# Key-by-receptance products of a delta-rule branch made once, before the solve, and read back from DRAM; output tiles reordered; recurrence one tile later

## The chip, the cores and the metric

One core of one Trainium2 chip. The metric is the device time of one execution in microseconds (us). The core has a matrix engine (PE, whose weight loads are listed as PEld), DVE (vector), ACT (scalar), POOL (GpSimd) and SP, which here only issues DMAs; ACT issues DMAs too.

## The reference

Two layers of a hybrid encoder trunk over 1024 prompt tokens and 8 samples of 16 tokens, T = 1152 tokens in all. In each layer one projection of the normalised input, `z = rmsnorm(x) @ W_in` (1024 to 24 tiles of 128 columns), feeds four branches: A (RWKV-7 time mixing, 4 heads of 64), B (latent attention), C (spatial gating) and D (trailing means); their outputs are gated and go through `W_out`. The change lies in branch A:

```python
def step(s, inp):                       # s: 64 x 64 state of a head
    r_t, w_t, k_t, v_t, kk_t, a_t = inp
    sa = einsum('bhij,bhj->bhi', s, -kk_t)
    s = s * w_t + sa (x) (kk_t * a_t) + v_t (x) k_t
    return s, einsum('bhij,bhj->bhi', s, r_t)
```

## The kernel before, in words

Tokens stand in three groups g of 384 columns; the last group ends with the samples. `project` makes one output tile f of W_in: per group 24 matmuls 128x384 (8 pieces of the contraction, 3 passes of split float32), so 72 for a tile. They read `xh`, `xl` and the weights `wh`, `wl` and fill one of two PSUM buffers `pj`. Below, n is the number of projection matmuls of the layer issued so far: tile number x 72. `F_ORDER` gives the order of the tiles. Behind each group a sink on ACT and DVE takes `pj` away: the token shift of the key, receptance and value tiles (K0, K1, R0, R1, V0, V1: two heads each), `windows` and `silu` for branch D (D0, GD0, D1, GD1).

All else is written as generators that wait in lanes. `tick()` advances each lane by one step, at the places `ticks` within a group and at its end. A scheduler then fixes one order of instructions for each engine, and an engine keeps to its order: what waits holds up all that stands behind it.

Branch A replaces the scan by 18 chunks of 64 tokens, 0 to 15 of the prompt, 16 and 17 of the samples:
- `a_elem(i, g)` makes, for head pair i, the tiles `kb` (both kinds of key divided by decay) and `ar` (the negated key times decay, and the decay, which `receptance` multiplies by r later).
- `systems(g)` makes for each chunk the key-by-key products (`pn`, 4 matmuls 64x64x64, listed as 8 each of 64x64), masks them on DVE into `ns` (two buffers) and writes them to DRAM, `nd` or `nds`, with a DMA on ACT (L514, L515).
- `solve()` loads them in another layout (L528, L529), inverts the unit triangular matrices in a long row of DVE pairs (L538, L540; first 15 pairs for the samples, then 31 pairs for the prompt), and writes the inverses to `dd` (L552, L553, on ACT).
- `recurrence()` goes through chunks 16, 17, 0, 1, ... 15. `prepare(c)` loads the inverse `tt` on SP, makes the key-by-receptance products (four 64x128x128 matmuls into `pg`, 8 listed), masks them on DVE into `Gm` (two buffers, L580), and makes all that does not need the state; `pz` (tt x Gm) is its first product on an inverse. `advance(c)` takes the state through the chunk.

The first 64 columns of the key-by-receptance product, which come from `ar`'s negated key, hold the key-by-key products.

Of the kernel before, what the change touches and what calls it, by code (L numbers as in the profile page):

```python
# [31 lines left out]
(WDAD, K0, R0, V0, K1, R1, V1, D0, GD0, D1, GD1, VC0, VC1, U0, GC0, U1, GC1,  # L32
 GB0, GB1, Q0, Q1K, CK, GA0, GA1) = range(NF)

F_ORDER = (WDAD, K0, K1, R0, R1, V0, V1, D0, GD0, D1, GD1, VC0, VC1, U0, GC0, U1, GC1,
           Q0, Q1K, CK, GB0, GB1, GA0, GA1)


# [10 lines left out]
def tile_trunk(ctx: ExitStack, tc: tile.TileContext, *aps):  # L49
# [60 lines left out]
    def s_tile(tag, bufs, cols=G):  # L110
        return sp_.tile([128, cols], F32, tag=tag, name=nm(tag), bufs=bufs)
# [7 lines left out]
    def pb():  # L119
        return ps_b.tile([128, 512], F32, tag="b", name=nm("b"))  # L120
# [36 lines left out]
    def gcols(g):  # L157
        return slice(g * G, (g + 1) * G)
# [163 lines left out]
    def halves(name, n, cols):  # L322
        return dr.tile([n, 128 * cols + 64], F32, tag=name, name=nm(name))
# [21 lines left out]
    for l in range(L):  # L345
# [13 lines left out]

        def inproj(f, sink):  # L360
            ticks = (3,)
            if f in (K1, R0, R1, V0, V1, D0, GD0, D1, GD1, VC0, VC1, GC0, U1, GC1,
                     GA0, GA1):
                ticks = (2, 5)
            elif f in (U0, GB0, GB1):
                ticks = (1, 3, 5)
            project([(l, f)], xh, xl, [sink], ticks)

# [36 lines left out]
        def shifted(f, dest, after=None):  # L405
            inproj(f, shift_sink(f, dest, after))
# [17 lines left out]
        def chv(t):  # L424
            return t.rearrange("p (c s) -> p c s", s=64)
# [63 lines left out]
        def receptance(i, fr):  # L489
            def after(g, zs):  # L490
                ex = AR[i][g][:, :, 1, :]
                Po.tensor_tensor(out=ex, in0=chv(zs), in1=ex, op=ALU.mult)
            shifted(fr, lambda g: s_tile("gn", 3), after)

        def values(fv):
# [2 lines left out]
            vfm.append(v)  # L498


        nd, nds = halves(f"nd{l}", 32, 64), halves(f"nds{l}", 4, 64)

        def hp(h):
            return slice(64 * (h % 2), 64 * (h % 2) + 64)

        def systems(g):
            for cl in range(6):
                c = 6 * g + cl
                pn = pb()[:, 0:128].rearrange("p (i t) -> p i t", i=2)
                for h in range(4):  # L510
                    mm(pn[hp(h), h // 2, :], KB[h // 2][g][hp(h), cl, h % 2, :], AR[h // 2][g][hp(h), cl, 0, :])
                ns = chp.tile([128, 2, 64], F32, tag="u0", name=nm("ns"), bufs=2)
                mk = cm[:, C_MP if c < 16 else C_MS, 0:64]
                V.tensor_tensor(out=ns, in0=pn, in1=mk.unsqueeze(1).broadcast_to([128, 2, 64]), op=ALU.mult)  # L514
                A.dma_start(out=whole(nd, c, 64) if c < 16 else whole(nds, c - 16, 64),  # L515
                            in_=ns.rearrange("p i t -> p (i t)"))
                if cl % 2:
                    yield

        def solve():  # L520
            NT = m_tile(1024).rearrange("p (s t) -> p s t", s=32)
# [38 lines left out]
        def prepare(c):  # L560

            g, cl = divmod(c, 6)
            samp = c >= 16
            if c == 16:
                St["Ss"] = m_tile(1024).rearrange("p (i s v) -> p i s v", i=2, s=NS)
                SY.dma_start(out=St["Ss"], in_=S0[l])
            tt = chp.tile([128, 2, 128], F32, tag="tt", name=nm("tt"), bufs=2)
            if samp:
                SY.dma_start(out=tt[:, :, 0:64], in_=whole(dds, c - 16, 64).rearrange("x s (i t) -> x s i t", i=2))
            else:  # L570
                SY.dma_start(out=tt.rearrange("p i t -> p (i t)"), in_=whole(dd, c, 128))

            Gm = chp.tile([128, 2, 2, 128], F32, tag="gm", name=nm("gm"), bufs=2)
            for hh in range(2):
                pg = pb()[:, 0:256].rearrange("p (i t) -> p i t", i=2)
                pr = slice(64 * hh, 64 * hh + 64)
                for i in range(2):
                    mm(pg[:, i, :], KB[i][g][pr, cl].rearrange("p a t -> p (a t)"),
                       AR[i][g][pr, cl].rearrange("p a t -> p (a t)"))
                V.tensor_tensor(out=Gm[:, hh], in0=pg,  # L580
                                in1=cm[:, C_MS if samp else C_MP, :].unsqueeze(1).broadcast_to([128, 2, 128]),
                                op=ALU.mult)

            pt = pb()
            for i in range(2):
                PE.transpose(pt[:, i * 128:(i + 1) * 128], KB[i][g][:, cl].rearrange("p a t -> p (a t)"), ident)  # L586
            for i in range(2):
                PE.transpose(pt[0:64, 256 + i * 128:256 + (i + 1) * 128], vfm[i][:, c * 64:(c + 1) * 64], ident)  # L588
            kbt = chp.tile([128, 256], F32, tag="kbt", name=nm("kbt"), bufs=2)
            A.activation(out=kbt, in_=pt[:, 0:256], func=AF.Copy)  # L590
            pvv = pt[0:64, 256:512].rearrange("p (i x v) -> p i x v", i=2, x=2)
            vu = chp.tile([128, 4, 64], F32, tag="vu", name=nm("vu"), bufs=2)
            vuv = vu.rearrange("p (i x) v -> p i x v", x=2)
            for hh in range(2):
                A.activation(out=vuv[64 - 64 * hh:128 - 64 * hh, :, hh, :], in_=pvv[:, :, hh, :], func=AF.Copy)
            yield

            if samp:
                if c == 16:

                    pys = pb()
                    pv4 = pys.rearrange("p (i s a t) -> p i s a t", i=2, s=NS, a=2)
                    for s in range(NS):
                        for h in range(4):
                            rhs = AR[h // 2][2][hp(h), 4 + s // 4, :, 16 * (s % 4):16 * (s % 4) + 16]
                            mm(pv4[hp(h), h // 2, s], St["Ss"][hp(h), h // 2, s, :], rhs)
                    ysm = m_tile(512)
                    St["YS"] = YS = ysm.rearrange("p (i a t) -> p i a t", i=2, a=2)
                    for a in range(2):
                        A.activation(out=YS[:, :, a, :].rearrange("p i (s t) -> p i s t", s=NS),  # L610
                                     in_=pv4[:, :, :, a, :], func=AF.Copy)
                yield
            else:
                pz = pb()
                for h in range(4):
                    o = 64 * (h % 2)
                    mm(pz[o:o + 64, h // 2 * 32:h // 2 * 32 + 32], Gm[o:o + 64, h % 2, h // 2, 0:64],
                       tt[o:o + 64, h // 2, 64:96])
                A.activation(out=zt[:, 0:64], in_=pz[:, 0:64], func=AF.Copy)
                yield  # L620
            pmv = pb()[:, 0:128].rearrange("p (i v) -> p i v", i=2)
            for h in range(4):
                q = slice(64 - 64 * (h % 2), 128 - 64 * (h % 2))
                mm(pmv[hp(h), h // 2, :], Gm[q, h % 2, h // 2, 0:64], vu[q, h, :])
            if not samp:
                pt2 = pb()
                for h in range(4):
                    o = 64 * (h % 2)
                    mm(pt2[o:o + 64, h // 2 * 32:h // 2 * 32 + 32], zt[o:o + 64, h // 2 * 32:h // 2 * 32 + 64],
                       tt[o:o + 64, h // 2, 32:64])  # L630
                for hh in range(2):
                    o = 64 * hh
                    A.activation(out=tt[o:o + 32, :, 32:64],
                                 in_=pt2[o:o + 32, 0:64].rearrange("p (i t) -> p i t", i=2), func=AF.Copy)
            u0 = chp.tile([128, 2, 64], F32, tag="u0", name=nm("u0"), bufs=2)
            A.activation(out=u0, in_=pmv, func=AF.Copy)
            St[c] = (tt, Gm, kbt, vu, u0)
# [266 lines left out]

        def after_k1(g, zs):
            start("a", a_elem(1, g, zs))
            if g > 0:
                go("a", systems(g - 1))

        project([(l, WDAD), (l, K0)], xh, xl,  # L910
                [shift_sink(WDAD, lambda g: z6[:, gcols(g)], tanh_part),
                 shift_sink(K0, lambda g: zk0[:, gcols(g)], lambda g, zs: start("a", a_elem(0, g, zs)))])
        shifted(K1, lambda g: zk1[:, gcols(g)], after_k1)
        go("a", idle(4))
        go("a", systems(2))
        go("a", idle(4))
        go("a", solve())
        receptance(0, R0)
        receptance(1, R1)
        values(V0)  # L920
        values(V1)
        A.dma_start(out=shift_o[l], in_=sho)
        pool_in(0, D0)
        go("a", recurrence())
        pool_gate(0, GD0)
        pool_in(1, D1)
        pool_gate(1, GD1)
        gating()
# [634 lines left out]
```

## Time and profile before

| | us |
|---|---|
| median of 3 runs | 1454.72 (1450.95 to 1456.58) |
| profiled execution | 1454.34 |
| its span | 1452.5 |
| PE busy in the span | 1373.0 (95%) |
| DVE / ACT / POOL busy | 783.5 / 740.7 / 437.7 |

The profiled execution is 1.8 us longer than its span, and its mean granted TensorE clock is 0.987 of full. Times in a trace count from the span's start. Layer 0's branch A stands between 50 and 361 us; layer 1 repeats it some 716 us later.

### The profile page before, as it was taken

To read this page: it belongs to the slowest core of one execution; us is meant where nothing else is said; L and a number is where in the kernel's file an instruction comes from. 1 tells how busy PE (TensorE), PEld (TensorE's weight loads), DVE (VectorE), ACT (ScalarE), POOL (GpSimd) and SP (SyncE) were. 2 spreads that over 40 slices of the span, in tenths; PEclk is the share of its full clock that TensorE was granted. 3 is DMA by queue.
4 is the path that set the end of the run, shared out by engine and by line. 5 is a ranking of instruction groups with operands and counts; after the bars stand their busy time and mean duration, and the time that the engine had idled before them with its cause. 6 is when DMAs were issued, how large, how long until landed. Compare 5 with 4: busy or idle time off the path is not lost. (4 is left out here: it accounts for less than half of the span.)

```text
span 1452.5 us, 26772 instructions
## 1 busy us (share of the span) xinstructions
PE 1373.0 (95%) x9938; PEld 1154.8 (80%) x9938; DVE 783.5 (54%) x1762; ACT 740.7 (51%) x1985; POOL 437.7 (30%) x576
## 2 busy tenths in 40 slices
PE   4899889999999999999989998999999999999999
PEld 3678878888988876679977787788799788666998
DVE  6985944445236557742287858543532474767211
ACT  6772244555366667642257521555643776666210
POOL 4514414336411110322162333332652111112320
PEclk9999999999999999999989999999999999999999
DMA  7213241110312114033301123221022111131232
GB/s 221 52 34 79 56 102 49 56 45 31 103 34 77 53 35 132 3 119 98 88 22 30 50 64 71 85 71 48 31 74 66 58 57 54 44 102 44 70 98 76
DMA packets 116594, 97.38 MB, mean 67 GB/s; under 512 B 46128, under 2 KB 111344, under 8 KB 116464
## 3 DMA queue, kind: packets, MB, share of 16 engines
q1 hardware_dynamic: 76776, 73.74, 17.6%
q10 hardware_dynamic: 39688, 21.94, 5.0%
q8 instruction: 78, 1.28, 0.4%
q14 instruction: 52, 0.43, 0.1%
HBM read 71.48 MB, written 24.16 MB: 66 GB/s over the span
## 5 line engine op out<-in xcount | busy, mean ns | idle before, releaser
L76 PE MATMUL pj<-xh,wh 128*128 128x384 f32 x1152 | 413.8, 360 | 18.0 <-ACT xh L280 7.3
L76 PE MATMUL pj<-xl,wh 128*128 128x384 f32 x1152 | 395.5, 343 | 3.7 <-POOL xl L282 2.7
L76 PE MATMUL pj<-xh,wl 128*128 128x384 f32 x1152 | 395.4, 343 | 0.0
L242 POOL TENSOR_TENSOR wl<-wr,wh 128x256 fp32r<-128x256 f32 x200 | 156.2, 789 | 463.8 <-ACT wh L241 387.5
L76 PEld LDWEIGHTS pj<-xh,wh 128*128 128x128 f32 x1152 | 220.7, 192 | 40.7 <-ACT sho L400 10.0
L76 PEld LDWEIGHTS pj<-xl,wh 128*128 128x128 f32 x1152 | 221.1, 192 | 11.2 <-POOL xl L282 4.7
L76 PEld LDWEIGHTS pj<-xh,wl 128*128 128x128 f32 x1152 | 220.7, 192 | 6.1 <-issue 4.8
L76 PE MATMUL pj<-yh,wh 128*128 128x384 f32 x384 | 130.0, 339 | 2.7 <-DVE x L1386 2.7
L76 PE MATMUL pj<-yh,wl 128*128 128x384 f32 x384 | 129.2, 337 | 0.0
L76 PE MATMUL pj<-yl,wh 128*128 128x384 f32 x384 | 129.0, 336 | 0.0
L241 ACT ACTIVATE wh<-wr 128x256 fp32r<-128x256 f32 x200 | 80.9, 414 | 86.0 <-PE pj L76 41.5
L76 PEld LDWEIGHTS pj<-yh,wh 128*128 128x128 f32 x384 | 72.5, 189 | 4.0 <-DVE x L1386 3.0
L242 POOL TENSOR_TENSOR wl<-m,wh 128x256 fp32r<-128x256 f32 x56 | 43.6, 788 | 103.7 <-ACT wh L241 76.4
L76 PEld LDWEIGHTS pj<-yl,wh 128*128 128x128 f32 x384 | 72.6, 189 | 0.1
L76 PEld LDWEIGHTS pj<-yh,wl 128*128 128x128 f32 x384 | 72.6, 189 | 0.1
L1261 ACT ACTIVATE X<-b,ng 128x512 f32<-128x512 f32 (+3 forms) x96 | 55.0, 576 | 28.7 <-DVE ng L1253 25.0
L76 PEld LDWEIGHTS st<-X,X 128*64 128x64 f32 x576 | 35.5, 136 | 31.6 <-DVE mx L1249 6.3
L76 PE MATMUL b<-sp,cr 128*128 128x384 f32 (+3 forms) x192 | 59.2, 389 | 1.0 <-POOL sp L99 0.6
L1249 DVE TENSOR_REDUCE mx<-b 128x1 f32<-128x512 f32 (+3 forms) x96 | 53.0, 552 | 8.5 <-PE b L76 6.9
L1382 DVE TENSOR_TENSOR pt<-pj,pt 128x384 f32<-128x384 f32 x24 | 13.4, 557 | 80.6 <-PE pj L76 80.6
L241 ACT ACTIVATE wh<-m 128x256 fp32r<-128x256 f32 x56 | 22.5, 413 | 62.2 <-PE pj L76 61.1
L76 PE MATMUL st<-X,X 128*64 128x128 f32 x576 | 53.3, 283 | 0.3
(296 smaller groups left out, 2558.1 us busy)
## 6 DMA issues: line engine op xcount, KB each, us to landing
wr<-in_win_dram SPq DMA_DIRECT2D x176, 128.0 KB
m<-in_wout_dram SPq DMA_DIRECT2D x12, 512.0 KB
x<-in_xT_dram SPq DMA_DIRECT2D x12, 384.0 KB
ysp<-m ACTq DMA_DIRECT2D x24, 192.0 KB
pt<-in_xT_dram SPq DMA_DIRECT2D x24, 192.0 KB
ea<-ysp SPq DMA_DIRECT2D x24, 192.0 KB
x1d<-x ACTq DMA_DIRECT2D x24, 192.0 KB
pt<-x1d SPq DMA_DIRECT2D x24, 192.0 KB
```

What stands on the lines that cost most here:

```text
L76: return PE.matmul(out, lhsT=lhsT, rhs=rhs, start=start, stop=stop, skip_group_check=True)
L241: A.activation(out=h, in_=r, func=AF.Copy)
L242: Po.tensor_tensor(out=lo, in0=r, in1=h.bitcast(F32), op=ALU.subtract)
L1249: V.tensor_reduce(out=mx[:, b:b + 1], in_=pc[:, :w], axis=AX.X, op=ALU.max)
L1261: A.activation(out=P[:, :w], in_=pc[:, :w], func=AF.Exp, scale=SCALE, bias=ng, accum_out=sums[pr][:, b, s, h:h + 1])
L1382: V.tensor_tensor(out=xr, in0=ps, in1=xr, op=ALU.add)
```

## The change

`systems(g)` now makes the whole key-by-receptance product of each chunk, masks it into `Gm`, writes its key-by-key part to `nd`/`nds` (two DMAs, one for each half) and the whole (256 KB) to a new DRAM tile `gd`, all three on SP. `prepare(c)` loads `Gm` from there on SP. The `pn` products, their mask and their DMA on ACT are gone. As the product needs `ar` with r in it, `systems(g)` starts behind `receptance(1, R1)`, one chunk for each step of the lane. To have r early the tiles are reordered: K0, V0, R0, K1, R1, V1 in place of K0, K1, R0, R1, V0, V1. The recurrence enters its lane after GD0 in place of before it, and D1 and GD1 get a third tick.

```diff
-F_ORDER = (WDAD, K0, K1, R0, R1, V0, V1, D0, GD0, D1, GD1, VC0, VC1, U0, GC0, U1, GC1,
+F_ORDER = (WDAD, K0, V0, R0, K1, R1, V1, D0, GD0, D1, GD1, VC0, VC1, U0, GC0, U1, GC1,
...
         def receptance(i, fr):
             def after(g, zs):
                 ex = AR[i][g][:, :, 1, :]
                 Po.tensor_tensor(out=ex, in0=chv(zs), in1=ex, op=ALU.mult)
+                if i == 1:
+                    go("a", systems(g))
...
+        gd = dr.tile([18, 128, 512], F32, tag=f"gd{l}", name=nm("gd"))
...
         def systems(g):
             for cl in range(6):
                 c = 6 * g + cl
-                pn = pb()[:, 0:128].rearrange("p (i t) -> p i t", i=2)
-                for h in range(4):
-                    mm(pn[hp(h), h // 2, :], KB[h // 2][g][hp(h), cl, h % 2, :], AR[h // 2][g][hp(h), cl, 0, :])
-                ns = chp.tile([128, 2, 64], F32, tag="u0", name=nm("ns"), bufs=2)
-                mk = cm[:, C_MP if c < 16 else C_MS, 0:64]
-                V.tensor_tensor(out=ns, in0=pn, in1=mk.unsqueeze(1).broadcast_to([128, 2, 64]), op=ALU.mult)
-                A.dma_start(out=whole(nd, c, 64) if c < 16 else whole(nds, c - 16, 64),
-                            in_=ns.rearrange("p i t -> p (i t)"))
-                if cl % 2:
-                    yield
+                samp = c >= 16
+                Gm = chp.tile([128, 2, 2, 128], F32, tag="gm", name=nm("gm"), bufs=2)
+                mk = cm[:, C_MS if samp else C_MP, :]
+                for hh in range(2):
+                    pg = pb()[:, 0:256].rearrange("p (i t) -> p i t", i=2)
+                    pr = slice(64 * hh, 64 * hh + 64)
+                    for i in range(2):
+                        mm(pg[:, i, :], KB[i][g][pr, cl].rearrange("p a t -> p (a t)"),
+                           AR[i][g][pr, cl].rearrange("p a t -> p (a t)"))
+                    V.tensor_tensor(out=Gm[:, hh], in0=pg, in1=mk.unsqueeze(1).broadcast_to([128, 2, 128]),
+                                    op=ALU.mult)
+                for hh in range(2):
+                    half = nds[2 * (c - 16) + hh] if samp else nd[2 * c + hh]
+                    SY.dma_start(out=half[0:128 * 64].rearrange("(s i t) -> s i t", s=64, i=2),
+                                 in_=Gm[64 * hh:64 * hh + 64, hh, :, 0:64])
+                SY.dma_start(out=gd[c], in_=Gm.rearrange("p h i t -> p (h i t)"))
+                yield
...
             Gm = chp.tile([128, 2, 2, 128], F32, tag="gm", name=nm("gm"), bufs=2)
-            for hh in range(2):
-                pg = pb()[:, 0:256].rearrange("p (i t) -> p i t", i=2)
-                pr = slice(64 * hh, 64 * hh + 64)
-                for i in range(2):
-                    mm(pg[:, i, :], KB[i][g][pr, cl].rearrange("p a t -> p (a t)"),
-                       AR[i][g][pr, cl].rearrange("p a t -> p (a t)"))
-                V.tensor_tensor(out=Gm[:, hh], in0=pg,
-                                in1=cm[:, C_MS if samp else C_MP, :].unsqueeze(1).broadcast_to([128, 2, 128]),
-                                op=ALU.mult)
+            SY.dma_start(out=Gm.rearrange("p h i t -> p (h i t)"), in_=gd[c])
...
-        shifted(K1, lambda g: zk1[:, gcols(g)], after_k1)
-        go("a", idle(4))
-        go("a", systems(2))
-        go("a", idle(4))
-        go("a", solve())
-        receptance(0, R0)
-        receptance(1, R1)
-        values(V0)
+        values(V0)
+        receptance(0, R0)
+        shifted(K1, lambda g: zk1[:, gcols(g)], after_k1)
+        receptance(1, R1)
+        go("a", solve())
         values(V1)
         A.dma_start(out=shift_o[l], in_=sho)
         pool_in(0, D0)
-        go("a", recurrence())
         pool_gate(0, GD0)
+        go("a", recurrence())
         pool_in(1, D1)
         pool_gate(1, GD1)
```

What it does to the order of instructions, at three places of layer 0 (the first number of a row is its place on its engine; line numbers of the changed kernel are 11 higher in the solve and 3 higher behind it).

PE in `systems`, before (some 290 projection matmuls of the layer have been issued): `b` is the PSUM tile of `pn`, two chunks in a row.

```order
299 L76 MATMUL pj_1046<-xh_332,wl_708 128x384
300 L76 MATMUL b_1098<-ar_564,kb_563 64x64 x2
301 L76 MATMUL b_1098<-ar_847,kb_846 64x64 x2
302 L76 MATMUL b_1106<-ar_564,kb_563 64x64 x2
303 L76 MATMUL b_1106<-ar_847,kb_846 64x64 x2
304 L76 MATMUL pj_1114<-xh_405,wh_663 128x384
```

PE in `systems` in the changed kernel, near n = 450: `b` is now `pg`, two of them for a chunk.

```order
452 L76 MATMUL b_1300<-ar_442,kb_441 128x128
453 L76 MATMUL b_1300<-ar_1025,kb_1024 128x128
454 L76 MATMUL pj_1336<-xh_406,wl_971 128x384
455 L76 MATMUL pj_1336<-xh_406,wh_970 128x384
456 L76 MATMUL b_1304<-ar_442,kb_441 128x128
457 L76 MATMUL b_1304<-ar_1025,kb_1024 128x128
458 L76 MATMUL pj_1336<-xl_407,wh_970 128x384
459 L76 MATMUL pj_1336<-xh_406,wl_971 128x384
460 L76 MATMUL pj_1336<-xh_406,wh_982 128x384
461 L76 MATMUL pj_1336<-xl_407,wh_982 128x384
462 L76 MATMUL pj_1336<-xh_406,wl_983 128x384
463 L76 MATMUL b_1325<-ar_442,kb_441 128x128
```

The products come 160 matmuls later in the layer, are two of 128 columns for each half of a chunk, and stand in smaller groups between the projections.

DVE at the end of the solve, before: L538 and L540 are its last pair, L655 is a step of sample chunk 16, L759 the last step of `silu` and L666 the sample chunks' masks.

```order
294 L538 TENSOR_TENSOR m_1395<-m_1394,m_1393 128x31
295 L540 TENSOR_TENSOR m_1394<-m_1394,m_1395 128x31
296 L550 COPY m_1393<-m_1394 128x1024
297 L655 TENSOR_TENSOR u_380_1954<-b_1956,u_380_1954 128x128
298 L580 TENSOR_TENSOR gm_1964<-b_1965,cm 128x256
299 L759 TENSOR_TENSOR pt_1940<-pj_1856,pt_1940 128x384
300 L580 TENSOR_TENSOR gm_1964<-b_1969,cm 128x256
301 L820 SCALAR_TENSOR_TENSOR m_1717<-st_1945,vcs,pt_1940 128x384
302 L759 TENSOR_TENSOR pt_2045<-pj_1983,pt_2045 128x384
303 L820 SCALAR_TENSOR_TENSOR m_1717<-st_2050,vcs,pt_2045 128x384
304 L666 TENSOR_SCALAR m_2000<-vu_1886,mseq_t 128x256 x4
```

DVE at the same place in the changed kernel, where L549 and L551 are the last pair, L794 is a window of D1, L669 the sample chunks' masks and L762 the last step of `silu`:

```order
318 L549 TENSOR_TENSOR m_1724<-m_1723,m_1722 128x31
319 L551 TENSOR_TENSOR m_1723<-m_1723,m_1724 128x31
320 L561 COPY m_1722<-m_1723 128x1024
321 L794 SCALAR_TENSOR_TENSOR m_2049<-pt_2169,pinv_t,m_2048 64x384
322 L794 SCALAR_TENSOR_TENSOR m_2049<-pt_2171,pinv_t,m_2048 64x384
323 L794 SCALAR_TENSOR_TENSOR m_2049<-pt_2286,pinv_t,m_2048 64x384
324 L794 SCALAR_TENSOR_TENSOR m_2049<-pt_2288,pinv_t,m_2048 64x384
325 L794 SCALAR_TENSOR_TENSOR m_2049<-pt_2434,pinv_t,m_2048 64x256
326 L794 SCALAR_TENSOR_TENSOR m_2049<-pt_2436,pinv_t,m_2048 64x256
327 L794 SCALAR_TENSOR_TENSOR m_2049<-pt_2445,pinv_t,zsm_2050 64x128
328 L669 TENSOR_SCALAR m_2188<-vu_2080,mseq_t 128x256 x4
```

Before, the windows of branch D that fell into the solve (those of D0) were worked between its pairs. Now eight windows of D1 stand behind its end, ahead of the masks of chunk 16 (L669).

PE at the end of the solve, before, from the last sample product on an inverse to the first prompt one (`b<-tt,gm`), and the projections that follow:

```order
747 L588 MATMUL b_2071<-cm,m_1373 64x128
748 L588 MATMUL b_2071<-cm,m_1544 64x128
749 L76 MATMUL b_2097<-u_395_2037,tt_1962 64x64 x4
750 L76 MATMUL b_2109<-tt_2060,gm_2062 64x32 x4
751 L76 MATMUL pj_2081<-xh_405,wh_1679 128x384
752 L76 MATMUL pj_2081<-xl_406,wh_1679 128x384
753 L76 MATMUL pj_2081<-xh_405,wl_1680 128x384
754 L76 MATMUL pj_2081<-xh_405,wh_1697 128x384
```

PE at the same place in the changed kernel, at n = 768 (between the second and third group of GD1):

```order
904 L76 MATMUL b_2269<-tt_2237,gm_2239 64x32 x4
905 L76 MATMUL b_2292<-m_2264,kbt_2153 64x256 x4
906 L76 MATMUL b_2300<-gm_2146,vu_2155 64x64 x4
907 L76 MATMUL b_2300<-m_2122,cm 64x64 x4
908 L76 MATMUL b_2311<-vu_2248,gm_2239 64x64 x4
909 L76 MATMUL b_2316<-tt_2237,zt 64x32 x4
910 L589 MATMUL b_2342<-cm,kb_441 128x128
911 L589 MATMUL b_2342<-cm,kb_1024 128x128
912 L591 MATMUL b_2342<-cm,m_738 64x128
913 L591 MATMUL b_2342<-cm,m_1430 64x128
914 L76 MATMUL b_2364<-u_456_2323,tt_2237 64x64 x4
915 L76 MATMUL pj_2719<-xh_406,wh_1981 128x384
```

Before, 45 projection matmuls stand between the solve's last pair and the first prompt product, with the steps of chunks 16 and 17 among them. Now what is left of chunks 16 and 17 and the whole of chunk 0's first steps stand in 23 rows that hold no projection (892 to 914); 8 chunks follow with 4 to 7 projection matmuls between their steps, and the rest with about 24 each, as before.

## Rows read from the trace of the kernel before

**Rows 1.** The page: span, and busy time of each engine.
```profile
span 1452.5 us, 26772 instructions
...
PE 1373.0 (95%) x9938; PEld 1154.8 (80%) x9938; DVE 783.5 (54%) x1762; ACT 740.7 (51%) x1985; POOL 437.7 (30%) x576
```

**Rows 2.** Windows of layer 0: length, then busy time (x instructions) of each engine.
```profile
67.71:162.73 95.02, 88.01 (x549) 75.55 (x548) 70.35 (x173) 42.38 (x112) 29.74 (x41) 0.99 0.21 56
...
177.64:202.37 24.73, 18.37 (x159) 15.45 (x156) 15.18 (x39) 6.95 (x22) 2.06 (x4) 0.93 0.43 80
```

**Rows 3.** The same view for `pj` instructions alone; the second stretch is pure projection.
```profile
67.71:162.73 95.02, 74.33 (x384) 66.83 (x384) 10.95 (x22) 11.53 (x38) 0.99 0.21 56
...
650.00:700.00 50.00, 50.00 (x290) 50.00 (x289) 6.69 (x12) 0.00 (x0) 1.00 0.36 101
```

**Rows 4.** PE groups of 67.71:162.73: count, busy us, mean ns, idle before.
```profile
L76 PE MATMUL b<-ar,kb 64*64 64x64 f32 x144 | 7.9, 228 | 2.2 <-DVE ns L514 1.9 <-DVE kb L481 0.3
...
L76 PE MATMUL st<-m,wlo 64*128 64x384 f32 x8 | 3.6, 535 | 0.0
...
L76 PE MATMUL st<-ea,cr 128*128 128x384 f32 x8 | 3.4, 511 | 0.0
...
L76 PE MATMUL b<-m,wlo 64*128 64x384 f32 x5 | 2.6, 594 | 0.0
```

**Rows 5.** What PE waited for, whole run: us, times, longest.
```profile
PE b L76 <- DVE gm L580: 6.2, 4, 2.9
```

**Rows 6.** PE timeline, two chunks of `systems` between projections: start, us.
```profile
121.44 0.34 PE L76 MATMUL pj<-xh,wl 128*128 128x384 f32 x1
...
121.71 0.68 PE L76 MATMUL b<-ar,kb 64*64 64x64 f32 x16
...
122.32 0.45 PE L76 MATMUL pj<-xh,wh 128*128 128x384 f32 x1
...
122.61 0.34 PE L76 MATMUL pj<-xl,wh 128*128 128x384 f32 x1
```

**Rows 7.** PE timeline, one chunk of the recurrence in its later part.
```profile
300.02 0.45 PE L76 MATMUL b<-vu,kbt 128*64 128x64 f32 x8
...
302.84 0.72 PE L76 MATMUL b<-ar,kb 64*128 64x128 f32 x8
...
303.49 0.44 PE L586 MATMUL b<-cm,kb 128*128 128x128 f32 x2
...
308.01 0.45 PE L76 MATMUL b<-vu,kbt 128*64 128x64 f32 x8
```

**Rows 8.** DVE timeline, the mask of the key products, two chunks apart.
```profile
119.50 0.29 DVE L514 TENSOR_TENSOR ns<-b,cm 128x128 f32<-128x128 f32 x1 [1.46 <-DMA nd<-ns]
...
123.01 0.29 DVE L514 TENSOR_TENSOR ns<-b,cm 128x128 f32<-128x128 f32 x1 [1.56 <-DMA nd<-ns]
```

**Rows 9.** DVE group of the masks in the recurrence.
```profile
L580 DVE TENSOR_TENSOR gm<-b,cm 128x256 f32<-128x256 f32 x72 | 28.3, 417 | 6.6 <-PE b L76 6.6
```

**Rows 10.** ACT timeline, the issue of one 192 KB write.
```profile
358.66 0.33 ACTq L899 DMA_DIRECT2D ysp<-m  x1
```

**Rows 11.** DMA view of 355:362, 40 slices of 0.175 us: what the engines moved.
```profile
GB/s 0 0 0 0 0 0 0 0 0 0 0 0 0 0 0 0 0 0 0 0 0 0 0 0 0 61 377 377 290 65 94 0 0 0 0 0 0 0 0 0
```

**Rows 12.** The tile `nd`, 90:140: ns minimum, median, maximum of the issue.
```profile
L515 ACTq DMA_DIRECT2D nd<-ns x16: 487/502/1078, 98.5 to 128.5; - x16
```

**Rows 13.** Timelines of four engines: the solve, from load to first use.
```profile
132.73 0.62 SPq L528 DMA_DIRECT2D m<-nd  x1
...
184.44 0.22 DVE L540 TENSOR_TENSOR m<-m,m 128x31 f32<-128x31 f32 x1
...
189.25 1.48 ACTq L553 DMA_DIRECT2D dd<-m  x1
...
201.78 0.37 PE L76 MATMUL b<-tt,gm 64*64 64x32 f32 x8
```

**Rows 14.** Windows: the stretch right behind an idle PE.
```profile
183.00:186.40 3.40, 3.34 (x15) 0.50 0.26 29
```

More of the change, by code (lines that the diff above doesn't have):

```diff
@@ L361, in inproj @@
             ticks = (3,)
-            if f in (K1, R0, R1, V0, V1, D0, GD0, D1, GD1, VC0, VC1, GC0, U1, GC1,
+            if f in (K1, R0, R1, V0, V1, D0, GD0, VC0, VC1, GC0, U1, GC1,
                      GA0, GA1):
                 ticks = (2, 5)
-            elif f in (U0, GB0, GB1):
+            elif f in (D1, GD1, U0, GB0, GB1):
                 ticks = (1, 3, 5)
@@ L906, in after_k1 @@
             start("a", a_elem(1, g, zs))
-            if g > 0:
-                go("a", systems(g - 1))
         project([(l, WDAD), (l, K0)], xh, xl,
@@ L923, in tile_trunk @@
         pool_in(0, D0)
+        pool_gate(0, GD0)
         go("a", recurrence())
-        pool_gate(0, GD0)
         pool_in(1, D1)
```

## The prediction

> **What bounds the kernel now.** I read the page first. PE is busy for 1373.0 of 1452.5 us, DVE and ACT for little more than half [rows 1], so the span is PE's row of instructions with its holes, and every edit is priced by what it adds to that row or to a hole in it. Busy time alone misleads: a matmul's record overlaps the next. In pure projection 290 of them fill 50 us, so one costs 50 / 290 = 0.172 us [rows 3], whatever its record says. Then I went to the stretches of layer 0 that the change touches, and read each as its length less its projections. From 67.71 to 162.73 us (n = 144 to 528) there are 384 projections, 66.2 of 95.0 us [rows 2, 3]; 28.8 us are something else. From 177.64 to 202.37, around the end of the solve, PE is busy for 18.37 of 24.73 us, so it is idle for 6.4, the largest hole of the layer [rows 2]. The two layers have the same shapes; I price one and double it.
>
> **1. The key products go.** Between the projections that start at 121.44 and 122.61 lie two chunks of them. Two projections of that 1.17 us are 0.34, so two chunks cost 0.82 and one 0.41 [rows 6]; 18 cost **7.4 us** a layer. Their busy time, 7.9 us [rows 4], says the same. Their DVE mask and DMA go too; neither engine bounds PE there beyond the wait in step 3.
>
> **2. The receptance products move.** One chunk takes PE from 302.84 to 303.49, 0.65 us, in the recurrence [rows 7]. In `systems` it takes the same, but it stands alone between projections, where the first matmul behind a group holds its place for 0.29 us instead of 0.172 (122.32 to 122.61, [rows 6]): 0.12 more. At most 18 such places make 2.1 us; some chunks share a place, so I take **+1.6**.
>
> **3. Waits in `systems`.** Before, a chunk waits for the write of `ns` two chunks earlier; this holds PE for 1.9 + 0.3 us in layer 0 [rows 4], because a buffer of `ns` comes back only after 123.01 - 119.50 = 3.5 us, which with two buffers is 1.75 us a chunk [rows 8]. That goes, **-2.2**. In its place DVE waits for the three writes out of a `Gm` buffer, and behind it on DVE stand the sinks that free `pj`; behind the writes on SP stand weight loads. The trace does not show this wait; I bound it. A buffer's turn is two masks, 2 x 0.42 [rows 9], then an issue of 0.50 for the second half [rows 12], then the 256 KB write. A 192 KB write was issued at 358.66 and its data ended at slice 30 of the view, 360.4, at up to 377 GB/s [rows 10, 11]: 1.75 us, and 64 KB more at that rate make 1.9. The turn is 3.25 us, and with two buffers a chunk 1.6 us. PE meanwhile has 116 / 18 = 6.4 projections and a product for each chunk, 1.1 + 0.65 = 1.76 us. So the lower bound is no wait. The upper one starts from what the 64 KB write's turn measured, 3.5 us, and adds two issues of 0.5 and the second mask of 0.42: 4.9, or 2.5 us a chunk, 0.7 behind PE, 13 us a layer. The direct sum is the nearer, the queue of weight loads speaks for something: **+2.0**.
>
> The Trainium skill speaks against the change here: "DMA: Bandwidth & Descriptors", section "Anatomy of one DMA", gives a fixed cost of about 2.0 us plus bytes at 436 GB/s, dominated by the receipt of the write in DRAM. As an estimate from that page 256 KB take 2.6 us, the turn 3.9, a chunk 1.97 and the layer +3.8; the whole sum would be 3.6 us higher. The trace's 1.75 us to the end of the data leaves the receipt out, so it does not contradict the page.
>
> **4. K0 to K1 loosened.** The 28.8 us are the key products (7.4), the low-rank products (3.6 + 3.4 + 2.6 = 9.6, [rows 4]), the 2.2 of step 3, and 9.6 more: sinks that free `pj` late while DVE works on `a_elem`, and restarts. DVE is busy 70 of those 95 us [rows 2]. V0 and R0 now stand between the two sets of element work, so PE has 144 plain projections, 25 us, while DVE catches up. K1's own element work still meets R1. Nothing to all of the 9.6 goes; I take two thirds, **-6.4**.
>
> **5. Loads of `Gm`.** Each is 256 KB on SP, behind the inverse's load. In the later part of the recurrence a chunk takes 8.0 us (300.02 to 308.01, [rows 7]), and the load is issued 15 projections, 2.6 us, and some 2 us of other products ahead, against a transfer of 1.9. Hidden there. In the packed part (step 7) it may not be: **+1.0**, between 0 and 4. The wait on the mask, 6.2 us for both layers [rows 5], goes; it is part of the hole in step 6.
>
> **6. The hole at the end of the solve** is the largest cost. The solve's load is issued at 132.73 and its last pair ends at 184.66: 51.9 us of DVE and latency [rows 13]. In the changed kernel that load stands at n = 543. From there PE has 225 projections to n = 768, 38.8 us, and an estimated 10 us of small products (those of branch D and of chunk 16, by their groups in the trace). It arrives 3.1 us before the solve ends. Then the rows at n = 768 hold no projection: both `pj` buffers wait for `silu`, whose last step stands on DVE behind the solve and eight windows. Before, the way from the last pair to the first prompt product on an inverse took 201.78 - 184.66 = 17.1 us, through the writes of the inverses on ACT (issued until 190.7) and the sample chunks [rows 13]. PE's products on that way, counted from the same stretch without the receptance ones, are 6.9 us. Idle: 3.1 + 17.1 - 6.9 = 13.3, against 6.4 before: **+6.9**. A smaller loss hides in both: behind the hole at 179 to 183 the granted clock was 0.50, the 1.2 GHz level, for 3.4 us [rows 14]. I take it as equal.
>
> **7. Packing.** Chunks 0 to 7 now follow with 4 to 7 projections each, not 24. A chunk takes 8.0 us with 24 projections (4.1) and the product that has moved (0.65), so 3.2 us remain [rows 7]. With 6 projections that makes 4.3 us, a little above what the state's own steps take; I take **0**, between -2 and +5.
>
> **Sum.** -7.4 + 1.6 - 2.2 + 2.0 - 6.4 + 1.0 + 6.9 = -4.5 a layer, -9.0 in all. The profiled execution took 1454.3 us (its span and 1.8 us), 0.4 below the median: **1445.3 us**, 0.6% faster. A measurement tells this kernel's change from nothing at about 0.5%, 7.3 us.
>
> **Rivals.**
> - *The hole grows (slower).* If the solve ends 10 us later against PE than I have it, the hole is 23 us. DVE's pairs run beside POOL's windows of D0 and D1, which the new order puts there. From 4.5 us later the gain is gone, from 8.2 it is slower by 0.5%. Ten give 1445.3 + 20 = 1465. Against it: less other work is left for DVE in that stretch. 0.13.
> - *The receptance products were filling.* In the packed chunks PE waits for the state's chain; there the moved 0.65 us would have cost nothing, and doing it earlier costs 8 x 0.65 = 5.2 a layer: 1455.7, no change. For it: 4 to 7 projections are 0.7 to 1.2 us, little to hide a chain behind. Against it: PE's own products fill most of a chunk. 0.17.
> - *The three writes pace `systems`.* At 2.5 us a chunk they add 11 us to step 3: 1467; at the half of that 1456. The upper bound needs writes as slow as that of `ns`, whose 64 KB took as long as the 192 KB of step 3 and more. 0.10.
> - *More is won.* PE comes late enough to n = 768 for the hole to be as before, and the stretch of step 4 gives all of its 9.6 us: 1445.3 - 2 x (6.9 + 3.2) = 1425. 0.20.
> - The forecast, 1438 to 1453 by itself: 0.40.
>
> **How the numbers follow.** Faster by over 0.5%: most of the last but one (0.19) and some three quarters of the forecast (0.31), 0.50. Slower: most of the first (0.12), half of the third, and the tails, 0.20. Within 0.5%: 0.30. The range leaves a tenth at each end: 1425 to 1464, from the larger gain to just short of the grown hole.
>
> **What would show it.** Right: no 64x64 key products in the trace; 288 products of 64x128, as before; PE from n = 144 to 528 in about 95 us although it now holds the receptance products (66.2 + 9.6 + 11.7 + 1.6 + 2.0 + 3.2 = 94.3); a hole of 13 us behind the solve, which ends near the time when PE reaches n = 768, with `pj` released by `silu`; chunks of about 7.3 us in the later recurrence. Wrong: PE waiting on DVE's mask for `Gm`'s writes for more than 5 us a layer, a hole of 20 us or of 6, packed chunks above 5 us, or products waiting for `Gm`'s load for more than 4 us a layer.

## The result, and the profile after

The changed kernel takes 1489.3 us (median of 4 runs, 1488.5 to 1491.0) against 1454.7 (1451.0 to 1456.6) before: ratio 1.0245, 95% interval 1.0225 to 1.0265. It is 2.4% slower; the forecast was 0.6% faster, and the time lies above the range.

The page of the changed kernel, its span, busy times and PE's granted clock in 40 slices:

```profile
span 1487.0 us, 26360 instructions
...
PE 1385.8 (93%) x9650; PEld 1164.1 (78%) x9650; DVE 783.2 (53%) x1726; ACT 737.4 (50%) x1985; POOL 437.3 (29%) x576
...
PEclk9899998999999999999989999789989999999999
```

PE has 288 instructions less than in [rows 1] and is busy for 12.8 us more. Both its idle time (span less busy) and its busy time have grown, and the mean granted clock fell from 0.987 to 0.967. I split each span in three. *Idle* is span less PE busy. *Lost at half clock* is the sum, over windows of 1 us, of busy time x (1 - granted clock): it counts as if what PE did at 1.2 GHz took half as long at 2.4. That is a little too much, since projections start every 0.32 us at 0.50 (206 to 212 below) and every 0.172 us at 1.00 [rows 3]. *Work* is the rest. This table holds the main reading of every run below, each from one profiled execution:

| kernel (profiled run) | span | idle | lost at half clock | work |
|---|---|---|---|---|
| before | 1452.5 | 79.5 | 17.8 | 1355.3 |
| after | 1487.0 | 101.2 | 37.5 | 1348.3 |
| order_alone | 1475.0 | 93.2 | 32.6 | 1349.1 |
| old_tiles | 1483.9 | 101.4 | 40.9 | 1341.7 |
| old_tiles_rec_early | 1479.8 | 103.5 | 34.5 | 1341.8 |
| rec_early | 1483.6 | 100.6 | 34.0 | 1349.0 |
| rec_late8 | 1467.0 | 91.1 | 28.6 | 1347.3 |
| rec_late16 | 1462.9 | 89.2 | 25.8 | 1347.8 |
| rec_late22 | 1459.2 | 89.8 | 23.5 | 1345.9 |
| own_products | 1494.4 | 94.7 | 29.6 | 1370.1 |
| own_late16 | 1486.0 | 87.5 | 28.2 | 1370.4 |
| before_rec_early | 1469.5 | 91.5 | 26.0 | 1352.0 |
| order_late16 | 1465.7 | 91.1 | 23.1 | 1351.5 |
| old_tiles_late12 | 1462.6 | 93.8 | 24.8 | 1344.0 |
| late22_sp | 1451.1 | 81.5 | 25.4 | 1344.2 |
| late22_d1 | 1459.9 | 92.2 | 23.0 | 1344.6 |
| late22_sp_d1 | 1454.7 | 89.6 | 19.2 | 1345.8 |
| before_sp | 1455.3 | 77.1 | 25.8 | 1352.4 |

So the change did save work, 7.0 us; it lost 21.7 us to idle time and 19.7 to the half clock. Together this is 34.4 of the 34.5 us.

Where, in layer 0, is told by the windows of the changed kernel that answer to [rows 2] (n = 144 to 528, and from the end of the solve to the next projection), of all engines:

```profile
68.10:168.28 100.18, 97.01 (x550) 83.08 (x549) 61.11 (x131) 40.65 (x109) 26.56 (x37) 0.98 0.26 83
...
224.66:247.94 23.28, 11.97 (x118) 7.83 (x117) 14.04 (x26) 5.98 (x22) 5.97 (x10) 0.71 0.51 112
```

The first stretch takes 5.2 us more than before because it now holds the receptance products; PE's idle time in it fell from 7.0 to 3.2 us, so the loss is not there. The second is one hole: 23.3 us without a projection, PE idle for 11.3 of it and busy for the other 12.0, with a mean clock of 0.71 over the stretch. Its DVE, in the changed kernel's timeline:

```profile
224.44 0.22 DVE L551 TENSOR_TENSOR m<-m,m 128x31 f32<-128x31 f32 x1
224.69 1.03 DVE L561 COPY m<-m 128x1024 f32<-128x1024 f32 x1
225.64 3.21 DVE L794 SCALAR_TENSOR_TENSOR m<-pt,pinv_t,m 64x384 f32<-64x384 f32 x4
230.07 1.78 DVE L794 SCALAR_TENSOR_TENSOR m<-pt,pinv_t,m 64x256 f32<-64x256 f32 x2 [1.23 <-POOL pt L787]
...
233.48 1.12 DVE L669 TENSOR_SCALAR m<-vu,mseq_t 128x256 f32<-128x256 f32 x4
```

The solve's last pair ends at 224.66, the windows of D1 keep DVE until 233.5 (for 2.3 us of it DVE waits for POOL), and only then come chunk 16's masks. PE's own waits over the whole run say the same (us, times, longest):

```profile
PE st L76 <- DVE ea L170: 13.8, 4, 9.8
PE st L76 <- POOL m L800: 8.5, 2, 4.9
PE b L76 <- DVE m L669: 7.8, 2, 4.4
PE b L76 <- DMA gm<-gd: 7.4, 7, 1.6
...
PE b L76 <- DMA tt<-dd: 7.1, 2, 3.8
PE b L76 <- ACT m L613: 5.4, 2, 2.8
...
PE b L76 <- DVE gm L522: 2.8, 8, 0.5
```

The first stood there before, too (14.0 us). The second, the third and the wait for `tt` are the three steps of that hole, one in each layer; the wait of [rows 5] is gone.

The clock of PE, in windows of the changed kernel, around a smaller hole (PE idles for 2.8 us from 200.5 until a product of chunk 16 can start) and in the large one:

```profile
200.00:206.00 6.00, 1.76 (x18) 0.96 0.14 45
206.00:212.00 6.00, 6.00 (x25) 0.50 0.01 3
...
230.00:238.00 8.00, 3.56 (x41) 0.50 0.44 66
```

Behind 6 us in which PE was busy for 1.8, the clock stands at 0.50 for 6 us in which PE is never idle. Before, [rows 14] showed 3.4 us of this once at this place. In all, 2 x (1 - 0.967) x 1487 = 98 us of the span are at half clock, against 38.

### The profile page after: what moved, and what is told of

It reads as the page before. It is cut to its first block, busy times and chain, and to the rows that moved or that the text cites. A ratio compares the mean times of both kernels' runs of the same rounds, so it can differ in the third digit from the quotient of the medians.

```text
span 1487.0 us, 26360 instructions
## 1 busy us (share of the span) xinstructions
PE 1385.8 (93%) x9650; PEld 1164.1 (78%) x9650; DVE 783.2 (53%) x1726; ACT 737.4 (50%) x1985; POOL 437.3 (29%) x576
## 5 line engine op out<-in xcount | busy, mean ns | idle before, releaser
L76 PE MATMUL pj<-xl,wh 128*128 128x384 f32 x1152 | 399.8, 347 | 2.2 <-POOL xl L282 1.8
L76 PEld LDWEIGHTS pj<-xl,wh 128*128 128x128 f32 x1152 | 222.8, 193 | 11.7 <-POOL xl L282 3.3
```

What stands on the lines that cost most here:

```text
L76: return PE.matmul(out, lhsT=lhsT, rhs=rhs, start=start, stop=stop, skip_group_check=True)
```

## The experiments

Three theories stood at the start. *Theory 1*: the solve ends later in the layer while the recurrence is written for an earlier end, so its chunks pile up behind the solve without projections between them. *Theory 2*: the round trip of Gm through DRAM. *Theory 3*: the receptance products cost more where they now stand alone. In what follows n is as before, and the place where chunk 0 is *written* is the n at which `prepare(0)` is called when the program is made; from there on the scheduler can place its steps.

| kernel | chunk 0 written at n | solve ends at n | its first product ran at n | us |
|---|---|---|---|---|
| before | 624 | 603 | 639 | 1452 to 1455 |
| after | 684 | 768 | 768 | 1489.3 |
| rec_late8 | 732 | 769 | 798 | 1467.7 |
| rec_late16 | 780 | 768 | 822 | 1464.2 |
| rec_late22 | 825 | 793 | 834 | 1461.2 |
| before_rec_early | 552 | 592 | 600 | 1470.2 |

**The parts of the change, apart.** The first four kernels take one part each.

order_alone: the kernel before with the order alone.

```diff
-F_ORDER = (WDAD, K0, K1, R0, R1, V0, V1, D0,
+F_ORDER = (WDAD, K0, V0, R0, K1, R1, V1, D0,
...
+        values(V0)
+        receptance(0, R0)
         shifted(K1, lambda g: zk1[:, gcols(g)], after_k1)
...
         pool_gate(0, GD0)
+        go("a", recurrence())
```

> The kernel before with only the order of the change: tiles K0, V0, R0, K1, R1, V1, the recurrence entered behind GD0, three ticks in D1 and GD1; the small key products, their write on ACT and the receptance products inside the recurrence stay. Theory 1 (the solve ends later in the layer, so that the recurrence begins in a hole and is squeezed): the loss stays, 1475 to 1490 us, with a hole of over 15 us near n = 700 to 770. Theory 2 (the round trip of Gm through DRAM, its three writes a chunk and its loads, costs the time): near the kernel before, 1450 to 1460. Theory 3 (the receptance products cost more where they now stand): also 1450 to 1460.

Measured 1475.5 us, ratio 1.0157 (1.0142 to 1.0172): 23 of the 35 us are there although the products are still made twice. Chunk 0 is written at 684, the solve ends at 737.

old_tiles: the changed kernel with the old order of tiles.

```diff
-F_ORDER = (WDAD, K0, V0, R0, K1, R1, V1, D0,
+F_ORDER = (WDAD, K0, K1, R0, R1, V0, V1, D0,
```

> The changed kernel with the old tile order K0, K1, R0, R1, V0, V1; products once, Gm through DRAM, recurrence behind GD0. r of the second pair comes one tile earlier, so systems and solve start 72 projections, some 12 us, earlier, while the recurrence enters at the same place. Theory 1: the hole at the end of the solve shrinks by most of 12 us a layer, 1460 to 1472. Theory 2: the round trip is unchanged, 1483 to 1492. Theory 3: 1483 to 1492 too.

1484.7 us, 1.0224 (1.0202 to 1.0245). The solve ended earlier, at n = 701, and the loss stayed: my first form of theory 1, that its end alone matters, fails. Chunk 0 is written at 684 as in the changed kernel, here only 17 projections ahead of the solve's end and there 84.

old_tiles_rec_early: the same with the recurrence entered ahead of GD0.

```diff
+        go("a", recurrence())
         pool_gate(0, GD0)
-        go("a", recurrence())
```

> The changed kernel with the old tile order and the recurrence entered ahead of GD0 as before: the products-once part of the change alone. Theory 1: the recurrence begins about half a tile later than before the change, 1450 to 1465. Theory 2: 1480 or more. Theory 3 (each product alone between projections costs 0.3 us more than in the recurrence, 36 of them about 11 us, less the removed key products 15): about 1450.

1484.2 us, 1.0231 (1.0208 to 1.0253). A miss for theory 1 as I had put it. Chunk 0 is now written at 624 and the solve ends at 686, so chunks pile up here, too. But with the written place 17, 62 and 84 projections ahead of the solve's end the loss is 2.2 to 2.5% each time: this lead alone does not give the size of the loss.

rec_early: the changed kernel with that same move.

> The changed kernel with one line moved back: the recurrence enters its lane ahead of GD0. Theory 1 in the form that the place of the recurrence matters: the windows of D1 no longer stand ahead of the sample chunks, a few us a layer less, 1475 to 1485. Theory 1 in the form that the end of the solve alone matters, and theories 2 and 3: the solve ends where it did, 1486 to 1492.

1488.0 us, 1.0241 (1.0226 to 1.0257): no change. Entering the lane earlier moves nothing, since `solve` stands ahead in it; chunk 0 is written at 684 as before the move. The lever is the number of steps ahead of the recurrence, which the next kernels use.

**The pile.** rec_late16 and rec_late8 are the changed kernel with empty steps.

```diff
+        go("a", idle(16))
         go("a", recurrence())
```

> The changed kernel with 16 empty steps in the lane between the solve and the recurrence, so that chunk 0 is written at n = 780 instead of 684; the solve ended at n = 768 on the chip, and before the change chunk 0 was written at 624 against a solve that ended at 603. Theory 1 in its sharper form (the recurrence is written for a solve that ends earlier than it does; the chunks due until then pile up without projections between them, PE idles and its clock falls): 1450 to 1465, no stretch of packed chunks, PE idle and half-clock time near those before. Theory 2 (the round trip of Gm): little changed, 1480 to 1490, since writes and loads are the same. Theory 3 (the products cost more alone): about 1480, too.

> The same with 8 empty steps: chunk 0 is written at about n = 732, so about half of the chunks that piled up still do. Theory 1: between, 1465 to 1478. Theories 2 and 3: 1480 to 1490.

1464.2 us, 1.0092 (1.0070 to 1.0115), and 1467.7, 1.0110 (1.0083 to 1.0137). With nothing else touched, 22 us of the 35 come back by the ratios (25 by the medians): idle time falls by 12.0 us and the half clock's loss by 11.7, and the work is the same. Eight steps do most of it. Chunks 16 and 17 open the recurrence, so the empty steps move them along with chunk 0.

before_rec_early: the kernel before, the same fault put in. The solve pauses behind every fourth pair and not every third, so it takes fewer steps of the lane, and the recurrence enters ahead of D0; chunk 0 is then written 40 projections ahead of the solve's end.

```diff
-                    if s % 3 == 2:
+                    if s % 4 == 3:
...
+        go("a", recurrence())
         pool_in(0, D0)
-        go("a", recurrence())
```

> The kernel before with only the place of the recurrence changed: the solve takes fewer steps of the lane and the recurrence enters ahead of D0, so that chunk 0 is written at n = 552 instead of 624, some 50 to 70 projections ahead of the solve's end. Nothing of the change is in it. Theory 1: it alone makes the kernel slower, 1465 to 1485, with a hole and packed chunks behind the solve. Theories 2 and 3: no change, 1450 to 1458.

1470.2 us, 1.0137 (1.0108 to 1.0166): slower by 17.5 us with none of the change in it. Its window from the solve's end to the first prompt product on an inverse, and its largest wait there:

```profile
182.50:199.70 17.20, 8.83 (x75) 0.80 0.54 85
```

```profile
PE b L76 <- DVE m L666: 5.5, 1, 5.5
```

It is a hole of the same kind as in the changed kernel: half of 17 us idle (3.2 us of as long a stretch before), and PE waiting for the sample masks on DVE behind the solve (1.3 us at most before). That the written place costs time is shown from both sides; that it is the whole loss is not, as the last table of this section shows.

**The round trip.** own_products is the changed kernel without `gd`; own_late16 is rec_late16 without it. Both make the receptance products a second time in the recurrence.

```diff
-                SY.dma_start(out=gd[c], in_=Gm.rearrange("p h i t -> p (h i t)"))
...
-            SY.dma_start(out=Gm.rearrange("p h i t -> p (h i t)"), in_=gd[c])
+            for hh in range(2):
+                pg = pb()[:, 0:256].rearrange("p (i t) -> p i t", i=2)
...
```

> The changed kernel without gd: systems still makes and masks the whole product but writes only the key-by-key halves, and the recurrence makes the receptance products again, as before. PE does 36 products more, 0.65 us each, 23 us in all. Theory 2: what the round trip cost goes; if it is the whole loss, 1454 + 23 = 1477 or less. Theory 1: the pile stays and the products come on top, 1495 to 1512.

> rec_late16 without gd: no whole write and no load of Gm, and the recurrence makes its 36 products again, 0.65 us each, 23 us in all, which nothing need hide once no chunks pile up. If the round trip were free: 1464 + 23 = 1487. Each us below that is a us that the round trip costs; 1475 would say 12 us of it, 1464 or less that making the products twice is no worse than moving them.

1499.2 us, 1.0326 (1.0289 to 1.0363), and 1491.3, 1.0261 (1.0240 to 1.0282). Without a pile, 22.6 us more work make the kernel 25 us slower (1.0261 against 1.0092), so the writes and loads of Gm cost no more than the waits that come with making the products again: as the cause of the loss theory 2 falls. With the pile 21.8 us more work cost only 12 us (1.0326 against 1.0245); idle time and half clock fell by 14 there, as they would if part of the products filled its holes.

**What is left without the pile.** rec_late22 has 22 empty steps, order_late16 is order_alone with 16, old_tiles_late12 is old_tiles with 12.

```diff
+        go("a", idle(22))
         go("a", recurrence())
```

> The changed kernel with 22 empty steps ahead of the recurrence, 6 more than in rec_late16, so that chunk 0 is written at about n = 825, where its first product stood on the chip with 16. Theory 1 alone: what is left of the pile goes, 1455 to 1462. If the rest of the loss is another one (the round trip, and holes where silu and the sample chunks stand among the solve's pairs on DVE): 1462 to 1468, the same as with 16.

> order_alone (tile order and place of the recurrence, without the products made once) with 16 empty steps ahead of the recurrence. If the pile was its only loss: 1446 to 1454, as the work outside holes and slow clock was 6 us less than before. If the later solve costs in other holes too: 1455 to 1465.

> old_tiles (products once, Gm through DRAM, the old order of tiles) with 12 empty steps ahead of the recurrence: the products-once part alone without a pile. If it gains what the removed products are worth once nothing piles up: 1440 to 1452. If the round trip and the products standing alone eat it: 1455 to 1468.

1461.2 us, 1.0060 (1.0038 to 1.0081); 1467.9, 1.0107 (1.0086 to 1.0128); 1465.4, 1.0084 (1.0058 to 1.0111). Each part without its pile loses less, but none gains, and order_late16 lies above both of the ranges that I had for it. In rec_late22 ACT stands still behind the four writes of the inverses, and PE with it; ACT's timeline (the last three of the four) and then PE's:

```profile
233.44 1.73 ACTq L564 DMA_DIRECT2D dd<-m  x1
235.20 2.78 ACTq L563 DMA_DIRECT2D dd<-m  x1
238.02 1.84 ACTq L564 DMA_DIRECT2D dd<-m  x1
239.90 0.42 ACT L241 ACTIVATE wh<-wr 128x256 fp32r<-128x256 f32 x1 [8.41 <-DMA dd<-m]
```

```profile
236.93 0.34 PE L76 MATMUL pj<-xh,wl 128*128 128x384 f32 x1
241.03 0.69 PE L76 MATMUL b<-cm,m 64*64 64x64 f32 x8 [3.76 <-ACT m L613]
241.65 0.69 PE L589 MATMUL b<-cm,kb 128*128 128x128 f32 x2
```

Behind that hole the clock is at 0.50 (241 to 244), and a pair takes 0.69 us where [rows 7] have 0.44 for the same pair (L586 there). late22_sp gives these writes to SP, before_sp does so in the kernel before, late22_d1 sets tile D1 ahead of GD0, late22_sp_d1 does both.

```diff
-                A.dma_start(out=diagonal(dd, i, 32, 128), in_=DT[64 * i:64 * i + 64])
+                SY.dma_start(out=diagonal(dd, i, 32, 128), in_=DT[64 * i:64 * i + 64])
...
-F_ORDER = (WDAD, K0, V0, R0, K1, R1, V1, D0, GD0, D1, GD1,
+F_ORDER = (WDAD, K0, V0, R0, K1, R1, V1, D0, D1, GD0, GD1,
```

> rec_late22 with the four writes of the inverses a layer issued by SP instead of ACT. In rec_late22 ACT does no work from 231 to 240 us while they wait for the queue, and the first product of chunk 16 that needs ACT waits 3.8 us at half clock thereafter. If ACT held by these writes is part of what is left: 1450 to 1457. If not, or if SP's weight loads come late for it: 1459 to 1468.

> The kernel before with the same single change, the writes of the inverses on SP. Before, ACT stands from 184.7 to 190.7 behind them, and PE waited 1.3 us for ACT there. If ACT held by these writes costs time: 1447 to 1451. If not: 1452 to 1458.

> rec_late22 with tile D1 ahead of GD0, so that while the first half of the solve runs on DVE a tile is projected whose buffer is freed by a copy on ACT, not by the last step of silu on DVE. If silu behind the solve's pairs is part of what is left (waits of 4.4 us at n = 672 and 768, with half clock behind them): 1450 to 1457. If the wait only moves to GD0 in its new place: 1458 to 1464.

> Both changes to rec_late22. If both are what is left of the loss: 1442 to 1451, below the kernel before. If only one is: as that one. If neither: 1458 to 1466.

late22_sp: 1454.0 us, 1.0019 (1.0006 to 1.0032). late22_d1: 1462.0, 1.0066 (1.0051 to 1.0081). late22_sp_d1: 1456.5, 1.0030 (1.0020 to 1.0041). before_sp: 1457.0, 1.0029 (1.0016 to 1.0042). The held ACT was worth 6 us of what was left (1.0060 to 1.0019); D1 ahead of GD0 nothing. In late22_sp ACT works through the time in which SP issues the writes, and PE's longest wait there is gone (SP's timeline, one row of ACT's, and PE's largest wait that remains):

```profile
234.04 0.62 SPq L563 DMA_DIRECT2D dd<-m  x1
...
236.09 2.76 SPq L563 DMA_DIRECT2D dd<-m  x1
238.90 2.38 SPq L564 DMA_DIRECT2D dd<-m  x1
```

```profile
234.63 0.64 ACT L613 ACTIVATE m<-b 128x256 f32<-128x256 f32 x2
```

```profile
PE pj L76 <- DVE pt L762: 15.4, 4, 4.5
```

In the kernel before the same edit does not help; there PE waited 2.8 us for that product in the whole run, in rec_late22 8.8, and in before_sp it waits 6.5 us for the loads of the inverses, 0.5 without the edit. No version beats the kernel before. late22_sp is level with it within 0.3%: its work is 11.1 us less, its idle time 2.0 us more and its half clock's loss 7.6 us more. The waits for `silu`'s last step behind the solve's pairs (15.4 us, none of that size before) are its largest. D1 ahead of GD0 did not remove them (18.5 us in late22_d1, 16.8 in rec_late22), so what they cost stays open.

**Where the loss stands.** Idle time and the half clock's loss together, both layers, by stretch of the layer (us, from the same profiled executions; behind n = 1230 all chunks are done):

| stretch | before | after | rec_late16 | rec_late22 | late22_sp | order_alone | order_late16 |
|---|---|---|---|---|---|---|---|
| n = 144 to 528 | 17.5 | 8.6 | 8.7 | 8.9 | 8.8 | 9.9 | 9.8 |
| n = 528 to chunk 0's first product | 16.1 | 44.2 | 37.5 | 38.7 | 28.4 | 37.5 | 41.6 |
| from there to n = 1230 | 14.0 | 35.2 | 18.1 | 10.9 | 12.3 | 27.4 | 11.6 |

The changed kernel lost 21 us in the last row, and the written place alone brings all of it back (rec_late22; order_late16 against order_alone; old_tiles 34.7, old_tiles_late12 13.0). It lost 28 us in the row above, which hardly answers to the written place: some 6 come back in rec_late22, none in order_late16. Ten more go when ACT no longer issues the writes of the inverses (late22_sp). For the 12 that are left the waits for `silu` behind a solve that ends later in the layer are the likely cause; no run shows it.

## Why the prediction was wrong

**Bound, and step 1** held. The 64x64 key products are gone, and the work fell.

**Step 2** was mis-sized. The changed kernel's PE timeline in `systems`:

```profile
146.31 0.34 PE L76 MATMUL pj<-xh,wh 128*128 128x384 f32 x1
146.58 0.82 PE L76 MATMUL b<-ar,kb 64*128 64x128 f32 x8
147.32 0.44 PE L76 MATMUL pj<-xl,wh 128*128 128x384 f32 x1
147.60 0.34 PE L76 MATMUL pj<-xh,wl 128*128 128x384 f32 x1
```

The last row shown starts 1.29 us after the first; less two projections, 0.95 us for a chunk where the recurrence paid 0.65 [rows 7]. A group loses at both its ends, the projection ahead of it too (0.27 us to the next start in place of 0.17). For all 36 that would be 10.8 us, not 3.2. Work fell by 7.0 where steps 1 and 2 had 11.6, which with step 1's 14.8 leaves 7.8 for the moved products. Theory 3 is right, at this size: over half of step 1's gain goes there.

**Step 3** was right for PE: it waited 2.8 us for these masks in the whole run, 3.7 before. DVE waited, as bounded. Its waits from 125 to 175 us and SP's issues:

```profile
DVE gm L522 <- DMA gd<-gm: 15.2, 11, 2.5
```

```profile
142.28 1.16 SPq L526 DMA_DIRECT2D nd<-gm  x2
143.49 0.58 SPq L528 DMA_DIRECT2D gd<-gm  x1
```

The mask that this write releases starts at 145.88: 2.4 us from the issue, against my 1.9 and the 2.6 that I estimated from the Trainium skill ("DMA: Bandwidth & Descriptors", "Anatomy of one DMA"). The trace is nearer to that formula, which the section gives for DMAs issued by GpSimd and not by SP, than to my reading of the end of the data. It decided nothing, since PE's own 0.95 + 1.1 us a chunk are as long.

**Step 4** held roughly: of the 100.2 us from n = 144 to 528, 66.2 are projections, 9.6 low rank and 17.1 products, which leaves 7.3 for steps 3 and 4 together, forecast 5.2, before 11.8.

**Step 5**: PE waited 7.4 us for Gm's loads, not 2. own_late16 shows that they cost no more than making the products again.

**Step 6** priced the hole itself roughly rightly and what lies around it not. PE reached n = 768 at 224.75, 0.1 us behind the solve's end (forecast: 3.1 ahead); the first prompt product follows 18.3 us later (forecast 20.2), with 11.3 us idle (forecast 13.3). What failed is the sentence "I take it as equal" on the clock, and that it saw one hole where there were more: a product of chunk 16 made its own at n = 679, with the 6 us at half clock shown above. From n = 528 to chunk 0's first product idle time grew by 18.6 us in the two layers and the half clock's loss by 9.5, 28 in all, where the step had 13.8. Over the whole run the clock cost 19.7 us more, of the 35.

**Step 7** is the step that failed in kind. It took the packed chunks as a rearrangement at 0. The window from chunk 0's first product to chunk 6's, for `pj` alone:

```profile
243.10:276.00 32.90, 9.30 (x41) 6.76 (x41) 1.42 (x3) 0.49 (x1) 0.95 0.43 137
```

That is 5.5 us a chunk, above the 5 named as a sign of being wrong. Less 41 projections (7.1) it is 4.3, where [rows 7] less the moved product have 3.2 and the same six chunks before, from 201.8 to 251.7 us with 138 projections, 3.7. In idle time and half clock the changed kernel lost 12 us more than before in chunks 0 to 7 of the two layers and 9 more from there to n = 1230: 21, where steps 5 and 7 had 2. The forecast read where the chunks stood and counted PE's products, but not that they stood there because they were written 84 projections ahead of the solve's end. rec_late22 moves the written place alone and has less of this loss than the kernel before.

Added up, of the 44 us between forecast and measurement 19 are missing in steps 5 and 7, 14 in step 6, 5 in steps 1 and 2, and 4 in steps 3 and 4; the rest lies outside these stretches.

**The rivals.** "The hole grows" had the right sign by the wrong mechanism: the solve did not end later against PE. "The products were filling" is seen where the pile is (own_products) and not without it (own_late16). "The three writes" held DVE, not PE. That the program's own timing of the recurrence had to follow the solve was no rival of mine.

## What to carry to other kernels

Where a scheduler interleaves a chain written step by step with filler work, the place at which the chain is written must follow the chip's end of what it waits for: moving the solve 160 projections and the recurrence 60 made a pile that cost 21 us, where the products saved 7. Price a hole by its idle time and then by the clock behind it; over this run the change added 21.7 us of the first and 19.7 of the second. And a small product between large ones costs its own time and its two edges: 0.95 us here for 0.65.

## What the runs showed of the hardware that was not expected

Behind a stretch of 6 us in which PE was busy for 1.8 (200 to 206 above) the clock stood at 1.2 GHz for 6 us in which PE was never idle (206 to 212). In the large hole it stood there through the whole of 230 to 238, where PE was busy for 3.6 us. The issue of one 256 KB write of the inverses took its engine 0.6 to 2.8 us, and ACT did no work for 8.4 us around four of them in rec_late22, while the 256 KB write of Gm took SP 0.58.
